# Layer 1's attention put into a written order on three engines, with filler products dealt out by period

## The chip, the core and the metric

One core of one Trainium2 chip runs the whole kernel as one program. The metric is the device time of an execution in microseconds; three executions of the kernel before took 1047.85, 1050.26 and 1059.63 us (median 1050.26).

## The reference

A two-layer decoder trunk on 256 tokens of width 1024, batch 1, in float32. Each layer is half a SwiGLU feed-forward (FFN), a mixer, and another half FFN, each behind an RMS norm that is scaled and shifted from a conditioning vector. The change is in the mixer of layer 1, a sparse attention with 16 heads of 64 in two key/value groups and three branches:

```python
u = h @ in_w                      # q, then k and v of three branches, then gates
q_rope = rope_partial(q, pos)
# compressed branch: 15 blocks of 32 tokens, each through a small MLP
p_c = masked_softmax(q @ kcmp.T * scale, cmp_end <= t);      o_c = p_c @ vcmp
# selected and window branch: at 256 tokens both are causal over all keys
p_s = masked_softmax(q_rope @ ks.T * scale, k <= t);         o_s = p_s @ vs
p_w = masked_softmax(q_rope @ kw.T * scale, k <= t);         o_w = p_w @ vw
y = sum(gate[..., c] * o[c] for c in range(3)) @ out_w
```

With 256 tokens there are four selection blocks and sixteen may be selected, so the selection takes all that are causal; the window of 512 takes all as well.

## The kernel before

All activations lie transposed, channels on the 128 partitions and the 256 tokens along the free axis. Matrix products with weights use two parts of each operand, a rounded high part and the rest: `mm3` (L171) issues high x high, high x low and low x high, three TensorE (PE) products of 128x128 by 128x256. The weights come as tiles of 128x1024 floats by DMA into seven raw buffers (`Stream`, L55 to L114). `need(i)` splits all tiles up to i in the order of one list: ACT makes the high part `wh` (L86), DVE the low part `wl` (L90), and the next DMA is issued. Seven pairs of `wh` and `wl` exist, so a split waits until the tile seven places ahead of it has been used up.

The tile framework's scheduler orders the instructions of each engine. Inside `with in_order()` (L223) PE, DVE and ACT keep the order in which the code is written; two such blocks that follow each other can still be laid into one another by the scheduler.

The mixer of layer 1 (`mixer1`, L937) first projects keys, values, gates and query tiles 0 to 3 (tiles 0 to 7 hold two heads each, one of each group). `rope_q` turns a quarter of each query tile: a DMA gathers the turned rows into `zq`, PE multiplies them with `rot`, DVE takes three steps (L701 to L703), a DMA puts them into `nqr`. `cmp_scores` and `cmp_soft` make the compressed branch's scores and softmax for four tiles at once; `cmp_trans` transposes its weights into `pc`.

Then come eight units u, one per query tile. Both branches and both groups of a unit are worked on together, for two halves t of the queries:

- `score(u, t)`: two products of 64 rows, one per group g, into the banks `s0` or `s1`; two bf16 products add the causal mask; DVE takes the minimum `nm` (L1182). For t = 0 there are 128 keys per branch, for t = 1 there are 256.
- `exps(u, t)`: four exponentials on ACT with their sums (L1193).
- `weights(u)`: reciprocal and gates on DVE (L1198, L1201). `norm(u, t)`: one DVE multiplication (L1206).
- `turn(u, part)`: four transposes on PE into the one bank `pt` (L1215), and a copy into `th`: by ACT for part 0 (L1218), by DVE for parts 1 and 2 (L1220).
- `values(u)`: on PE the compressed values, then sixteen products of `th` with the values into the one bank `y`; then `y` is split into `yh` (ACT, L180) and `yl` (DVE, L181).

Between these stand filler products from a list `todo`: the projections of query tiles 4 to 7 (`q_step`, 96 products), their rotation and compressed softmax, then the output projection (`out_step(b, k)`, six products each, into four accumulators b) as soon as `y[k]` exists. `filler(n)` takes n units of cost from it. None of this is in order by hand: the scheduler decides. What is left of the output projection goes into `step`, called by the next FFN's `transition` (L388). That one is written in order: it first needs the next FFN's five weight tiles (L391), then updates `x` by pairs of accumulators.

Of the kernel before, what the change touches and what calls it, by code (L numbers as in the profile page):

```python
# [18 lines left out]
KD = 8  # L19
# [35 lines left out]
class Stream:  # L55
    def __init__(self, nc, pool, junk, cond, wst, mst, modraw, items, halved):
# [8 lines left out]
        self.n_free = 0  # L65
# [45 lines left out]
    def free(self, i):  # L111
        assert i == self.n_free
        del self.split[i]
        self.n_free += 1  # L114
# [3 lines left out]
def hybrid_trunk_kernel(ctx: ExitStack, tc: tile.TileContext, xT, c, wst, mst, prm_d, cst_d, wab_d, cw1_d, cw2_d,  # L118
# [818 lines left out]
    def mixer1(prev):  # L937
# [132 lines left out]
        def cmp_soft(w):  # L1070
# [8 lines left out]
            A.activation(out=sc, in_=sc, func=ACTF.Exp)  # L1079
            sm = ap.tile([P, 16], F32, tag="csm", name="csm", bufs=2)  # L1080
# [8 lines left out]
            return sc  # L1089
# [21 lines left out]
        sc0 = cmp_soft(0)  # L1111
        att = banks_att()
        late = {}

        def q_step(i, k):
            if k == 0:
                late["b"] = oa()
                late["w"] = st.need(p0 + 7 + i)
                st.need(p0 + 8 + i)
# [29 lines left out]

        todo = [(1, None, lambda i=i, k=k: q_step(i, k)) for i in range(4, 8) for k in range(KD)]  # L1150
        todo += [(1, None, lambda: rope_q(1, ap, oa())), (2, None, cmp1), (0, None, soft1)]
        outs = [(2, k, lambda b=b, k=k: out_step(b, k)) for k0 in (0, 4) for k in range(k0, k0 + 4) for b in range(2)]
        todo += [(1, None, lambda: cmp_trans(1, late["sc"], oa()))] + outs

        def filler(n):
            while todo and n > 0 and (todo[0][1] is None or todo[0][1] in y):
                cost, _, f = todo.pop(0)
                f()
                n -= cost
# [76 lines left out]
        score(0, 0)  # L1236
        exps(0, 0)
        score(0, 1)
        cmp_trans(0, sc0, att("pt", 1))
        filler(8)  # L1240
        for u in range(KD):
            more = 1 if u < 3 else 0
            exps(u, 1)
            if u + 1 < KD:
                score(u + 1, 0)
            filler(3 + more)
            weights(u)
            norm(u, 0)
            if u + 1 < KD:
                exps(u + 1, 0)  # L1250
                score(u + 1, 1)
            turn(u, 0)
            filler(2 + more)
            norm(u, 1)
            turn(u, 1)
            turn(u, 2)
            filler(3 + more)
            values(u)
        gate = gate_of(1, 1)
        params(1, 2)  # L1260
        banks_std()

        def step(b):
            if b == 0:
                filler(100)
                assert not todo
            if b > 1:
# [182 lines left out]
```

## Time and profile before

| | us |
|---|---|
| executions (3) | 1047.85, 1050.26, 1059.63 |
| profiled execution | 1049.2 |
| its span, first to last instruction | 1047.2 |
| granted clock of TensorE, mean | 0.993 of full |
| first score product to last product with the values | 749.83 to 833.81 |

The page lists busy times, shares in 40 slices, the chain of work that ended last, and groups of instructions. "<-" in a row names what was written from what, and a row of the chain gives its start, its length and the engine that held it. [...]

### The profile page before, as it was taken

Reading aid. Unit: us, or ns where it says so; the run is one execution under the profiler, and the core shown is the slowest. Engines: PE = TensorE matmul, PEld = TensorE weight load, DVE = VectorE, ACT = ScalarE, POOL = GpSimd, SP = SyncE. Lnnn points to the kernel's source line nnn. Section 1 sums busy time; section 2 is a strip of 40 time slices with the busy share of each in tenths; the row PEclk is TensorE's granted clock in tenths of the full one; section 3 lists DMA queues with packets and bytes.
Section 4 is the critical chain, followed back from the end, with each engine's and each line's share of the span. In section 5 each row is a group of like instructions: output and inputs, shape, how many; then the busy total and the mean of one; then the engine's idle time right before and its main releaser. Section 6 shows DMA issues by size and latency. Waiting matters only on the chain.

```text
span 1047.2 us, 20415 instructions
## 1 busy us (share of the span) xinstructions
PE 1007.5 (96%) x8102; PEld 961.2 (92%) x8102; DVE 806.8 (77%) x1380; ACT 550.5 (53%) x943; POOL 1.6 (0%) x14
## 2 busy tenths in 40 slices
PE   4999999999999999999999999999999999999997
PEld 2899999999889999999999999998865699999996
DVE  8979887899767988886788888779576578565654
ACT  5364444567966644444674444466744466444442
POOL 0000000000000000000000000000000000000000
PEclk9999999999999999999999999999989999999998
DMA  9989899948543799998359999843620036766611
GB/s 360 336 283 405 313 338 322 360 135 288 209 150 136 268 364 328 332 351 289 121 180 391 332 333 334 321 147 121 222 64 28 17 102 242 264 218 222 225 58 41
DMA packets 69728, 249.99 MB, mean 239 GB/s; under 512 B 8001, under 2 KB 9537, under 8 KB 69378
## 3 DMA queue, kind: packets, MB, share of 16 engines
q1 hardware_dynamic: 69346, 248.18, 66.8%
q8 instruction: 63, 1.03, 0.4%
q10 hardware_dynamic: 288, 0.52, 0.1%
q14 instruction: 31, 0.25, 0.1%
HBM read 245.39 MB, written 1.05 MB: 235 GB/s over the span
## 4 chain that ended last, share of the span: by engine, by line
PE 80%; DVE 10%; ACT 6%; issue 2%; DMA 1%; SPq 0%; ACTq 0%; DVEq 0%
PE ps L169 45%; PE oa L169 17%; PE ob L169 14%; DVE wl L90 2%; PE s L169 2%; PE y L169 2%; ACT wh L86 1%; DVE junk L94 1%; DVE t L460 1%; DVE HL L455 1%; PE pt L1215 1%; DVE x L383 1%; ACT HH L461 1%; DMA raw<-mst 1%; ACT p L1193 1%
## 5 line engine op out<-in xcount | busy, mean ns | idle before, releaser
L90 DVE TENSOR_TENSOR wl<-raw,wh 128x1024 fp32r<-128x1024 f32 (+1 forms) x339 | 384.0, 1147 | 119.6 <-ACT wh L86 118.6
L86 ACT ACTIVATE wh<-raw 128x1024 fp32r<-128x1024 f32 x315 | 328.1, 1055 | 219.2 <-PE ps L169 110.5
L169 PE MATMUL ps<-HL,wh 128*128 128x256 f32 (+1 forms) x1392 | 392.3, 282 | 2.4 <-DVE HL L455 2.4
L169 PE MATMUL ps<-HH,wh 128*128 128x256 f32 (+1 forms) x1392 | 391.7, 283 | 2.7 <-ACT HH L461 2.7
L169 PE MATMUL ps<-HH,wl 128*128 128x256 f32 (+1 forms) x1392 | 393.3, 283 | 0.6 <-DVE wl L90 0.4
L169 PEld LDWEIGHTS ps<-HH,wh 128*128 128x128 f32 x1392 | 262.9, 189 | 4.1 <-ACT HH L461 3.6
L169 PEld LDWEIGHTS ps<-HL,wh 128*128 128x128 f32 x1392 | 262.7, 189 | 3.1 <-DVE HL L455 2.9
L169 PEld LDWEIGHTS ps<-HH,wl 128*128 128x128 f32 x1392 | 264.1, 190 | 1.4 <-DVE wl L90 1.4
L94 DVE SCALAR_TENSOR_TENSOR junk<-raw,cond 128x1024 bf16<-128x1024 f32 x144 | 175.6, 1219 | 12.6 <-DMA raw<-mst 12.5
L169 PE MATMUL oa<-gl,wh 128*128 128x256 f32 x352 | 98.1, 279 | 0.2
L169 PE MATMUL oa<-gh,wh 128*128 128x256 f32 x352 | 98.0, 279 | 0.1
L169 PE MATMUL ob<-gl,wh 128*128 128x256 f32 x352 | 97.7, 278 | 0.1
L169 PE MATMUL oa<-gh,wl 128*128 128x256 f32 x352 | 97.7, 278 | 0.0
L169 PE MATMUL ob<-gh,wh 128*128 128x256 f32 x352 | 97.6, 278 | 0.0
L169 PE MATMUL ob<-gh,wl 128*128 128x256 f32 x352 | 97.5, 277 | 0.0
L180 ACT ACTIVATE gh<-g 128x256 fp32r<-128x256 f32 x82 | 33.6, 417 | 72.9 <-DVE g L489 72.9
L169 PEld LDWEIGHTS oa<-gh,wh 128*128 128x128 f32 x352 | 66.3, 189 | 0.5 <-ACT gh L180 0.5
L169 PEld LDWEIGHTS oa<-gl,wh 128*128 128x128 f32 x352 | 66.2, 188 | 0.5 <-DVE gl L181 0.5
L169 PEld LDWEIGHTS ob<-gl,wh 128*128 128x128 f32 x352 | 66.1, 188 | 0.3 <-DVE gl L181 0.3
L169 PEld LDWEIGHTS oa<-gh,wl 128*128 128x128 f32 x352 | 66.3, 188 | 0.0
L169 PEld LDWEIGHTS ob<-gh,wh 128*128 128x128 f32 x352 | 66.0, 188 | 0.1
L169 PEld LDWEIGHTS ob<-gh,wl 128*128 128x128 f32 x352 | 66.1, 188 | 0.0
(242 smaller groups left out, 1315.1 us busy)
## 6 DMA issues: line engine op xcount, KB each, us to landing
raw<-wst SPq DMA_DIRECT2D x315, 512.0 KB, 5.1
raw<-mst SPq DMA_DIRECT2D x144, 512.0 KB, 5.5
cw<-cw SPq DMA_DIRECT2D x1, 2048.0 KB, 7.6
x<-xT SPq DMA_DIRECT2D x1, 1024.0 KB, 5.2
nqr<-nqf SPq DMA_DIRECT2D x4, 192.0 KB, 3.2
cst<-cst SPq DMA_DIRECT2D x1, 721.0 KB, 7.8
wab<-wab SPq DMA_DIRECT2D x1, 512.0 KB, 4.1
out<-raw ACTq DMA_DIRECT2D x2, 256.0 KB, 3.0
```

The costliest lines, as they stand in the source:

```text
L86: nc.scalar.activation(out=h, in_=raw, func=ACTF.Copy)
L90: nc.vector.tensor_tensor(out=l[:, cols], in0=raw[:, cols], in1=h.bitcast(F32)[:, cols], op=ALU.subtract)
L94: nc.vector.scalar_tensor_tensor(out=self.junk, in0=raw, scalar=1.0, in1=self.cond, op0=ALU.mult, op1=ALU.mult, accum_out=self.modraw[i // ...
L169: PE.matmul(out, lhsT, rhs, start=start, stop=stop, skip_group_check=True)
L180: A.activation(out=h, in_=src, func=ACTF.Copy)
L383: V.scalar_tensor_tensor(out=x[:, d], in0=accs[d // 2][:, d % 2 * S:d % 2 * S + S], scalar=gate[:, d:d + 1], in1=x[:, d], op0=ALU.mult, op ...
L455: V.scalar_tensor_tensor(out=HL[:, k, 0:S], in0=ts.pop(k), scalar=shift[:, k:k + 1], in1=HH[:, k, 0:S].bitcast(F32), op0=ALU.add, op1=ALU. ...
L460: V.scalar_tensor_tensor(out=t, in0=x[:, k], scalar=amp[:, k:k + 1], in1=rbs, op0=ALU.mult, op1=ALU.mult)
L461: A.activation(out=HH[:, k, 0:S], in_=t, func=ACTF.Identity, bias=shift[:, k:k + 1])
L1193: A.activation(out=p[:, 2 * g + br], in_=s[:, g, br * n:br * n + n], func=ACTF.Exp, scale=-1.0, bias=nm[:, g, br:br + 1], accum_out=units[ ...
L1215: PE.transpose(pt[:, c * P:(c + 1) * P], p[:, c, o:o + P], ident)
```

## The change

The whole unit loop goes into one `in_order` block, in periods. Period u writes unit u's scores, minima and exponentials and, between them, unit u-1's transposes; then unit u's `weights` and both `norm`s; then unit u-1's `values`. There are nine periods, the last without a new unit. The fill of a period is a fixed list, cut into three parts: behind transposes 1, behind transposes 2, behind the values. Query tiles 4 to 7 take periods 0 to 2, all 96 products behind the first scores; rotation and compressed softmax period 3; output products the rest, two groups of six per period from period 5 on. The splits are dealt out too: `ahead` says up to which weight tile each period splits, ahead of its `weights`. `cmp_soft` is cut in two, so that the second set's normalization (`cmp_norm`) stands in the next period. Four groups of the third accumulator's output products (`out_step(2, 0..3)`) come behind the last values. Weight tiles may now be freed in any order.

```diff
--- before.py
+++ after.py
@@ -109,9 +108,7 @@
             assert self.step(), "stream blocked"
     def free(self, i):
-        assert i == self.n_free
         del self.split[i]
-        self.n_free += 1
@@ -1077,6 +1074,10 @@
             V.tensor_reduce(out=nmx, in_=sc16, axis=AX.X, op=ALU.max)
             V.tensor_tensor(out=sc16, in0=sc16, in1=nmx.unsqueeze(2).to_broadcast([P, 16, 16]), op=ALU.subtract)
             A.activation(out=sc, in_=sc, func=ACTF.Exp)
+            return sc
+
+        def cmp_norm(w, sc):
+            sc16 = sc.rearrange("p t h c -> p (t h) c")
             sm = ap.tile([P, 16], F32, tag="csm", name="csm", bufs=2)
             V.tensor_reduce(out=sm, in_=sc16, axis=AX.X, op=ALU.add)
             V.reciprocal(out=sm, in_=sm)
@@ -1086,7 +1087,6 @@
                 V.tensor_tensor(out=v, in0=v, in1=gt, op=ALU.mult)
             V.tensor_scalar(out=sm[:, 0:8], in0=sm[:, 0:8], scalar1=C("valid")[:, 0:1], scalar2=None, op0=ALU.mult)
             V.tensor_tensor(out=sc16, in0=sc16, in1=sm.unsqueeze(2).to_broadcast([P, 16, 16]), op=ALU.mult)
-            return sc
 
         def cmp_trans(w, sc, bank):
             scf = sc.rearrange("p t h c -> p (t h c)")
@@ -1109,6 +1109,7 @@
         V.tensor_tensor(out=vb4, in0=bv[:, 0:P].unsqueeze(1).to_broadcast([P, 4, P]),
                         in1=C("vsel").rearrange("p (a d) -> p a d", a=4), op=ALU.mult)
         sc0 = cmp_soft(0)
+        cmp_norm(0, sc0)
         att = banks_att()
         late = {}
 
@@ -1116,7 +1117,6 @@
             if k == 0:
                 late["b"] = oa()
                 late["w"] = st.need(p0 + 7 + i)
-                st.need(p0 + 8 + i)
             b = late["b"][:, 0:S]
             mm3(b, at(late["w"], k), hk(k), k == 0, k == KD - 1)
             if k == KD - 1:
@@ -1146,17 +1146,6 @@
                     k == KD - 1)
             if k % 4 == 3:
                 st.free(wo + i)
-
-        todo = [(1, None, lambda i=i, k=k: q_step(i, k)) for i in range(4, 8) for k in range(KD)]
-        todo += [(1, None, lambda: rope_q(1, ap, oa())), (2, None, cmp1), (0, None, soft1)]
-        outs = [(2, k, lambda b=b, k=k: out_step(b, k)) for k0 in (0, 4) for k in range(k0, k0 + 4) for b in range(2)]
-        todo += [(1, None, lambda: cmp_trans(1, late["sc"], oa()))] + outs
-
-        def filler(n):
-            while todo and n > 0 and (todo[0][1] is None or todo[0][1] in y):
-                cost, _, f = todo.pop(0)
-                f()
-                n -= cost
 
         def scores(u, t):
 
@@ -1233,39 +1222,63 @@
             y[u] = yy
             units[u].clear()
 
-        score(0, 0)
-        exps(0, 0)
-        score(0, 1)
-        cmp_trans(0, sc0, att("pt", 1))
-        filler(8)
-        for u in range(KD):
-            more = 1 if u < 3 else 0
-            exps(u, 1)
-            if u + 1 < KD:
-                score(u + 1, 0)
-            filler(3 + more)
-            weights(u)
-            norm(u, 0)
-            if u + 1 < KD:
-                exps(u + 1, 0)
-                score(u + 1, 1)
-            turn(u, 0)
-            filler(2 + more)
-            norm(u, 1)
-            turn(u, 1)
-            turn(u, 2)
-            filler(3 + more)
-            values(u)
+
+        qs = [lambda i=i, k=k: q_step(i, k) for i in range(4, 8) for k in range(KD)]
+
+        def o(b, k):
+            return lambda: out_step(b, k)
+
+        between = [qs[0:14], qs[14:24], qs[24:32] + [o(0, 0)], [lambda: rope_q(1, ap, oa()), o(0, 1), cmp1, soft1],
...
+        ahead = [2, 3, 5, 5, 5, 7, 7, 8, 8]
+
+        with in_order():
+            st.need(p0 + 12)
+            cmp_trans(0, sc0, att("pt", 1))
+            for u in range(KD + 1):
+                jobs = between[u]
+                n = len(jobs)
+                parts = [jobs[:n // 3], jobs[n // 3:2 * n // 3], jobs[2 * n // 3:]]
+
+                def fill(part):
+                    for f in parts[part]:
+                        f()
+
+                if u < KD:
+                    score(u, 0)
+                if u > 0:
+                    turn(u - 1, 0)
+                if u < KD:
+                    exps(u, 0)
+                    score(u, 1)
+                if u > 0:
+                    turn(u - 1, 1)
+                if u < KD:
+                    exps(u, 1)
+                fill(0)
+                if u > 0:
+                    turn(u - 1, 2)
+                fill(1)
+                st.need(p0 + 11 + ahead[u])
+                if u < KD:
+                    weights(u)
+                    norm(u, 0)
+                    norm(u, 1)
+                if u > 0:
+                    values(u - 1)
+                fill(2)
+            banks_std()
+            for k in range(4):
+                out_step(2, k)
         gate = gate_of(1, 1)
         params(1, 2)
-        banks_std()
 
         def step(b):
-            if b == 0:
-                filler(100)
-                assert not todo
-            if b > 1:
-                for k in range(KD):
+            if b < 2:
+                out_step(b, KD - 1)
+            else:
+                for k in range(4 if b == 2 else 0, KD):
                     out_step(b, k)
             if b == 3:
                 ap_.__exit__(None, None, None)
```

On PE, units 5 and 6 of the kernel before. `s_9836` is the score tile t = 0 of unit 5, `s_9865` that of t = 1; `y` is unit 4's values.

```order
L1215 MATMUL pt<-cst,p 128x128 x2
L169 MATMUL s_9836<-kf,nqr_8993 128x256 x2
L169 LDWEIGHTS identb
L169 MATMUL s_9836<-maskb,identb 128x256
L169 LDWEIGHTS identb
L169 MATMUL s_9836<-maskb,identb 128x256
L1215 MATMUL pt<-cst,p 128x128 x4
L169 MATMUL y<-th,nvp 64x256 x2
L169 MATMUL s_9865<-kf,nqr_8993 128x512
L169 MATMUL y<-th,nvp 64x128 x2
L169 MATMUL y<-th,nvp 64x256 x2
L169 MATMUL y<-th,nvp 64x128 x2
```

The two halves of `s_9865` (x2 where they stand together) are apart: one between the values, the other behind them.

On PE, the same place of the changed kernel: the masks of `s_9930` (unit 6, t = 0) to the fill behind transposes 2.

```order
L166 MATMUL s_9930<-maskb,identb 128x256
L1204 MATMUL pt<-cst,p 128x128 x4
L166 MATMUL s_9950<-kf,nqr_8993 128x512 x2
L166 LDWEIGHTS identb
L166 MATMUL s_9950<-maskb,identb 128x2x128
L166 LDWEIGHTS identb
L166 MATMUL s_9950<-maskb,identb 128x2x128
L1204 MATMUL pt<-cst,p 128x128 x8
L166 MATMUL oa<-yh,wh 128x256
```

The halves stand together, and transposes 1 and 2 follow each other (x8) with no fill between them in periods 5 to 8.

On PE, the head of the stretch in the kernel before, around the compressed scores (`ob<-kbd`); `oa<-HH,wh` and its like are products of query tiles 4 to 7.

```order
L169 MATMUL oa<-HH,wh 128x256
L169 MATMUL oa<-HL,wh 128x256
L169 MATMUL ob<-kbd,nqf_8990 128x32 x8
L169 MATMUL oa<-HH,wl 128x256
L169 MATMUL oa<-HH,wh 128x256
```

The same place of the changed kernel, from the last hidden-layer products (`x_9167`, `hid_9006`) to the first scores.

```order
L166 MATMUL ps<-x_9167,cw_9017 128x2x15 x4
L166 MATMUL ps<-hid_9006,cw_9002 128x32
L166 MATMUL ob<-kbd,nqf_8990 128x32 x8
L166 MATMUL ps<-cw_9002,hid_9306 128x128
L1094 MATMUL pt<-cst,sc 128x128 x2
L166 MATMUL s_9356<-kf,nqr_8992 128x256 x2
```

The 51 query products that stood around the compressed scores are gone from here, and the transpose of the compressed softmax (`pt<-cst,sc`) stands ahead of the first scores.

On DVE, the last unit of the kernel before, from its last minimum to the next FFN's splits.

```order
L1182 TENSOR_REDUCE nm<-s_10027 128x4
L1220 COPY th<-pt 128x4x128 x2
L1198 RECIPROCAL sm<-sm 128x8
L1201 TENSOR_TENSOR sm<-sm,gts 128x4 x2
L1206 TENSOR_TENSOR p<-p,sm 128x512
L1206 TENSOR_TENSOR p<-p,sm 128x1024
L181 TENSOR_TENSOR yl<-y,yh 128x256
L1220 COPY th<-pt 128x4x128 x2
L181 TENSOR_TENSOR yl<-y,yh 128x256
L90 TENSOR_TENSOR wl<-raw,wh 128x1024 x3
```

The same in the changed kernel, from the split that is written in period 7 to the last copy.

```order
L89 TENSOR_TENSOR wl<-raw,wh 128x1024
L1187 RECIPROCAL sm<-sm 128x8
L89 TENSOR_TENSOR wl<-raw,wh 128x1024
L1190 TENSOR_TENSOR sm<-sm,gts 128x4 x2
L89 TENSOR_TENSOR wl<-raw,wh 128x1024
L1195 TENSOR_TENSOR p<-p,sm 128x512
L1195 TENSOR_TENSOR p<-p,sm 128x1024
L178 TENSOR_TENSOR yl<-y,yh 128x256
L89 TENSOR_TENSOR wl<-raw,wh 128x1024
L1209 COPY th<-pt 128x4x128
L89 TENSOR_TENSOR wl<-raw,wh 128x1024
L1209 COPY th<-pt 128x4x128
```

Four splits of later tiles, which stood behind the last unit, are laid by the scheduler between the last unit's steps.

## Rows read from the trace of the kernel before

**Rows 1.** The page: the span, PE's busy time, its granted clock in 40 slices.
```profile
span 1047.2 us, 20415 instructions
...
PE 1007.5 (96%) x8102; PEld 961.2 (92%) x8102; DVE 806.8 (77%) x1380; ACT 550.5 (53%) x943; POOL 1.6 (0%) x14
...
PEclk9999999999999999999999999999989999999998
```

**Rows 2.** Windows of the stretch and its parts.
```profile
core 0: us, PE busy (x) PEld busy (x) DVE busy (x) ACT busy (x) POOL busy (x), PEclk, DMA share, GB/s
749.83:833.62 83.79, 78.15 (x488) 49.96 (x487) 57.57 (x104) 42.30 (x156) 0.00 (x0) 0.96 0.18 58
...
776.40:786.60 10.20, 8.68 (x47) 6.33 (x46) 6.51 (x15) 3.83 (x17) 0.00 (x0) 0.68 0.42 117
...
802.46:833.83 31.37, 28.74 (x196) 18.37 (x196) 20.46 (x35) 14.52 (x51) 0.00 (x0) 1.00 0.10 34
741.50:749.83 8.33, 8.33 (x72) 8.19 (x72) 2.15 (x6) 4.80 (x10) 0.00 (x0) 1.00 0.89 335
```

**Rows 3.** The chain that ended last: start us, length us, what.
```profile
775.62 0.37 ACT nqf L969
...
776.69 2.35 DMA zq<-nqf
...
798.28 1.94 ACT p L1193 x7
...
800.27 1.12 PE s L169 x2
...
802.41 1.05 PE s L169 x2
...
809.76 1.13 PE s L169 x4
...
824.24 0.67 PE pt L1215 x4
...
824.94 0.70 DVE th L1220
...
831.46 0.44 PE pt L1215 x4
831.90 1.91 PE y L169 x18
...
836.29 5.55 PE ob L169 x47
...
841.86 1.07 ACT wh L86
```

**Rows 4.** Instructions by shape, 749.83 to 833.62: busy us, mean ns, idle before.
```profile
L1182 DVE TENSOR_REDUCE nm<-s 128x4 f32<-128x1024 f32 x8 | 9.7, 1214 | 5.1 <-PE s L169 5.1
L1206 DVE TENSOR_TENSOR p<-p,sm 128x1024 f32<-128x1024 f32 x8 | 9.7, 1211 | 0.0
L90 DVE TENSOR_TENSOR wl<-raw,wh 128x1024 fp32r<-128x1024 f32 x7 | 8.5, 1220 | 3.1 <-ACT wh L86 3.1
...
L86 ACT ACTIVATE wh<-raw 128x1024 fp32r<-128x1024 f32 x6 | 6.2, 1051 | 2.6 <-PE oa L169 2.6
L1206 DVE TENSOR_TENSOR p<-p,sm 128x512 f32<-128x512 f32 x8 | 5.5, 692 | 0.0
```

**Rows 5.** Timeline of the head, and of a lone half of tile 0.
```profile
742.80 0.36 ACT L1101 ACTIVATE kbd<-ps 64x16 f32<-64x16 f32 x2
...
745.11 1.87 PE L169 MATMUL ob<-kbd,nqf 128*128 128x32 f32 x16
...
793.17 0.70 PE L169 MATMUL s<-kf,nqr 64*128 64x256 f32 x2
793.80 0.39 PE L169 MATMUL s<-maskb,identb 128*128 128x256 bf16 x2
```

More of the change, by code (lines that the diff above doesn't have):

```diff
@@ L64, in __init__ @@
         self.split = {}
-        self.n_free = 0
         self.done_m = set()
@@ new lines, in o @@
+        def o(b, k):
+            return lambda: out_step(b, k)
+        between = [qs[0:14], qs[14:24], qs[24:32] + [o(0, 0)], [lambda: rope_q(1, ap, oa()), o(0, 1), cmp1, soft1],
+                   [o(1, 0), lambda: cmp_norm(1, late["sc"]), o(1, 1), o(0, 2), o(1, 2), lambda: cmp_trans(1, late["sc"], att("pt", 1))]]
+        between += [[o(0, k), o(1, k)] for k in range(3, 7)]
+        ahead = [2, 3, 5, 5, 5, 7, 7, 8, 8]
[35 more added lines that the diff above has]
+                out_step(2, k)
```

## The prediction

> **What bounds the kernel now.** I read the page first, then the windows of the stretch, the chain of waits, the instructions by shape and the timeline. The page says that TensorE (PE) counts as busy for 96% of a span of 1047.2 us, at full granted clock but for one slice inside [rows 1]. The change touches one stretch, from the first score product at 749.83 to the last product with the values, which ends at 833.81 with its drain of 0.2 [rows 3]: 83.8 us, 8% of the span. There PE counts as busy for 78.2 us, DVE for 57.6, ACT for 42.3 [rows 2]. PE's figure says too much, since a product counts until its last column is out. Its work can be counted from dense rows. One of the 174 projection products that the changed stretch holds takes 5.55/47 = 0.118 us; a pair of score halves 0.63 us (tile 0) or 1.13 (tile 1), with masks some 0.78 and 1.27; four transposes 0.44; a unit's products with the values 1.9 [rows 3, 5]. Eight units: 8 x (0.78 + 1.27 + 3 x 0.44 + 1.9) = 42.2. 174 products: 20.5. Rotation, compressed scores and their transposes: some 2.5. Together 65 us. Whatever the order, the rest of the stretch is waits between PE, DVE and ACT, and that is what a new order can win or lose.
>
> Three things in the order of before cost PE time. A lone score half costs what the pair costs: 1.12 and 1.05 us for two instructions against 1.13 for four [rows 3], and 0.63 for a lone half of tile 0 (793.17 to 793.80) [rows 5]. Around the eighth query tile the chain leaves PE at 775.62: read-out, DMA issue and DMA until 779.04, 3.4 us [rows 3]. Soon after, the granted clock falls: it averages 0.68 over 776.40 to 786.60, so 10.2 x 0.32 = 3.3 us of PE time go [rows 2].
>
> **The change part by part.** *Score halves.* Nine of the sixteen score tiles of before have their halves apart, five large and four small; all stand together now. That is 5 x 1.05 + 4 x 0.63 = 7.8 us of PE time, won only where PE is what ends last.
>
> *Rotation.* The eighth query tile is now complete at the end of unit 2's period, and the rotation comes after unit 3's scores, about 3 us later. The trip of 3.4 us lies beside them almost whole, and the next transposes wait longer there anyway. I price it at nothing.
>
> *Head.* Before, 51 projection products (6.0 us) stood between the hidden-layer products at 741.5 and the first scores, beside ACT's table loads and the compressed softmax; PE was busy for all of that window [rows 2]. Now all 96 come after the first scores, and the first thing after the compressed scores is the transpose of the finished softmax. So the head is the bare chain: the keys are ready at 742.80 + 0.36, the compressed scores take 1.87 [rows 5], drain 0.2, and ten small operations of DVE and ACT follow, with ten hand-overs of 0.03 to 0.04 (as from 824.91 to 824.94 in rows 3). They are smaller than the 128x512 that takes 0.69 [rows 4], eight of them with 256 columns or fewer; I estimate 0.4 for each, 3.9 together, and put the first scores at 749.6. That is only 0.2 earlier than before, with 6.0 us of work still to do.
>
> *One period per unit.* In a period PE runs scores 0 of unit u, transposes 0 of u-1, scores 1, transposes 1, fill, transposes 2, fill, values of u-1, fill. Transposes 2 need the bank that DVE's copy 1 empties, and that copy stands on DVE behind the minimum over the large scores. Up to there the path is 0.78 + 0.44 + 1.27 + 0.2 drain + 1.21 (the minimum) + 0.69 (the copy) + 0.5 (transposes from a standstill), 5.1 us with hand-overs and with DVE's next instruction starting 0.08 before the last ends [rows 3, 4]; then 1.9 for the values, and 0.118 for each product placed behind transposes 2. A product before them is free up to 14 (PE waits 1.65 us there). So a period is 7.0 us plus its later fill.
> Unit 0: scores 2.05 and 42 products: 7.0.
> Unit 1: 7.0 + 21 x 0.118, and 1.2 of waiting: the split of a weight tile stands ahead of the softmax weights, and ACT's half of it behind the read-out of query tile 4. That is scores 2.05, 24 products 2.8, read-out behind the exponentials until 5.8, then 1.05 and 1.22 for the split [rows 4], 0.4 for reciprocal and gates, 0.69 for norm 0: 9.0, and PE is there at 7.8. So 10.7.
> Unit 2: 9.4. Unit 3: 6 products, compressed scores 1.87, and 0.5 from three rotation steps on DVE ahead of copy 2: 10.1. Unit 4: 18 products and two transposes, 9.3. Unit 5: 12 products, 8.5. Unit 6: the same plus 1.0, because two splits (ACT's half behind the exponentials) stand ahead of unit 5's norms: 9.5. Unit 7: 8.5. Sum 73.0.
>
> *Last unit.* DVE's queue in unit 7 is the worst place of the order. Besides the split written there, two of the next stage's stand between the reciprocal and the first norm, and two more between the copies. The large minimum ends 3.9 us into the period, the large exponentials take 1.94 [rows 3], and ACT's three halves end at 6.9, 7.9 and 8.9; DVE's end at 8.1, 9.4 and 10.7, norm 0 at 11.4. PE runs dry at 8.5, so it waits 2.8. Then transposes and copies come one by one with a split between them: about 1.4 (0.70 of transposes and 0.6 of the copy on ACT), 1.9, 1.4, and 1.9 for the values. So 9.4, and the values of unit 7 end 73.0 + 9.4 = 82.4 us after the first scores, at 832.0, against 833.6. Gain 1.6.
>
> *Tail.* The split that the next stage needs first (its fifth tile) waits for output products to free its buffer. It starts at 841.86 [rows 3], 8.25 after the values. Now 7 + 24 + 11 + 24 = 66 products stand there, the first 30 of which cover unit 7's read-out: 66 x 0.118 + 0.2 = 8.0. Gain 0.25. Behind it the order is as before.
>
> *Clock.* Not shown at the new places, so bounded. The rows show one fall, after the chain had been off PE for 3.4 us, and a loss of 3.3 us. The head now has 743.2 to 749.6 with 2.2 us of work, and the end of unit 7 some 6 us with four short groups. Each place costs between 0 (as in 802.46 to 833.83, where the clock stays at 1.00 [rows 2]) and 3.3. I take half, 1.65, at each: a fall that starts while nothing runs spends part of itself on nothing.
> [...]
>
> **The sum.** -1.6 - 0.25 + 3.3 = +1.45 on the profiled execution's 1049.2 us: 1050.7. That execution stands 1.1 below the median of the three runs (1050.26; 1047.85 to 1059.63).
>
> A cross-check: 7.8 (halves) + 3.4 (rotation) + 3.3 (clock) - 6.0 (head) = 8.5 us could be won. 82.4 - 65 = 17.4 us of waits in the new order stand against 83.8 less the old order's work, which is 65 - 5.3 (45 products fewer) + 7.8: 16.3, of which 6.7 were rotation and clock, so 9.6 against 17.4. That leaves 0.7, near the 1.6.
>
> **Rivals.**
> 1. *The clock holds at both places.* For it: PE never stands quite bare for longer than about 4 us; against it: the fall of before came after 3.4. 1049.2 - 1.85 = 1047.4.
> 2. *The clock is low through periods 5 to 7* (slower). Their fill is only 12 products, and PE waits 1.65 us in each 8.4 at the same place. If that is enough, 6.4 us of each path double in three periods (+19), and the time is about 1069. It decides from the point at which a window between 797 and 824 shows under 0.9. Against it: 802.46 to 833.83 held 1.00 with 28.7 of 31.4 counted busy [rows 2].
> 3. *The waits overlap*, because hand-overs are shorter than I count or the engines run further ahead: PE's own work becomes the bound. At the full 65 us the time is 1049.2 - 83.8 + 65 = 1030; half of the way 1039. Against it: the path of a period is a chain of dependent instructions with measured times.
> 4. *The second trip of the rotation is late.* Rotated queries go to unit 4 by DMA from DVE's last rotation step, 32.9 us after the start; with the first trip's 3.4 they are there at 36.3, and unit 4 starts at 37. If the trip is twice as long, 1050.7 + 2.7 = 1053.4.
> That the order isn't what it says is excluded, since the three engines' orders are listed; only the two blocks' overlap in the last unit departs from the written order, and it is priced.
>
> **How the numbers follow.** Forecast (the clock falls at one or both places) 0.62, own range 1046 to 1055. Rival 1: 0.20. Rival 2: 0.07. Rival 3 beyond 1%: 0.05. Rival 4: 0.06. About 1% (10.5 us) is what a measurement of this kernel can tell from no change. Faster comes from rival 3 alone: 0.05. Slower from rival 2 and a hundredth for a sum that fails elsewhere: 0.08. Within 1%: 0.87. The range takes in rival 1 with the last unit's splits harmless (1047.4 - 2.8 = 1044.6, so 1044) and both falls at 3.3 with rival 4 (1047.4 + 6.6 + 2.7 = 1056.7, so 1057).
>
> **What would show it.** Right: no lone score half; 82 to 87 us from the first scores to the last values; in each of periods 5 to 7 a wait of PE of 1.2 to 1.7 us for DVE's copy 1; 2 to 3 us before unit 7's first transposes, on the norm; a granted clock under 1 near 750 and near 830, and nowhere between. Wrong: a stretch under 78 us (the waits overlap), a fall between 760 and 820, unit 4's scores waiting for a DMA, or the fifth split starting much later than 8 us after the last values.

## The result, and the profile after

The changed kernel takes 1060.48 us (median of 20 executions, 1055.77 to 1068.07), the kernel before 1049.86 in the same comparison (20 executions). The ratio is 1.0096, 95% interval 1.007 to 1.0122: slower by about 1%, where the prediction said 1050.7 and a range up to 1057. (The ratio leaves disturbed executions out, such as one of before that took 3438 us; the medians here and below are over all.) The profiled execution took 1057.26 us, 3.2 below its median, as that of before stood below its own.

First the page of the changed kernel, for [rows 1]:

```profile
span 1055.4 us, 20400 instructions
...
PE 1001.9 (95%) x8102; PEld 961.2 (91%) x8102; DVE 807.5 (77%) x1380; ACT 549.7 (52%) x943; POOL 1.6 (0%) x14
...
PEclk9999999999999999999999999999799899999999
```

The span is 8.2 us longer while PE's busy time is 5.6 us shorter: the same 8102 instructions on PE run, and the lone score halves are gone as planned. So the loss must be standing time and clock. The clock row has a 7 where the head of the stretch lies and an 8 at the end of unit 7; before it had an 8 at the rotation and one in the last slice.

Now the stretch by periods: windows of the changed kernel from the first scores of one unit to those of the next; the eighth window ends where PE runs dry in unit 7, and the ninth with the values of unit 7. The three rows behind the dots are the first fall of the clock, the time between the falls, and the second fall. Columns as in [rows 2]: length, then busy time of each engine, then PEclk.

```profile
core 0: us, PE busy (x) PEld busy (x) DVE busy (x) ACT busy (x) POOL busy (x), PEclk, DMA share, GB/s
752.20:761.61 9.41, 9.41 (x55) 6.66 (x54) 2.53 (x3) 5.04 (x19) 0.00 (x0) 0.76 0.01 2
761.61:772.42 10.81, 9.74 (x73) 7.04 (x72) 8.42 (x16) 5.64 (x20) 0.00 (x0) 1.00 0.19 58
772.42:782.36 9.94, 9.53 (x73) 7.12 (x72) 7.12 (x12) 6.96 (x22) 0.00 (x0) 1.00 0.19 61
782.36:793.67 11.31, 8.79 (x67) 6.37 (x66) 8.74 (x16) 4.41 (x18) 0.00 (x0) 1.00 0.44 139
793.67:803.45 9.78, 9.01 (x70) 6.56 (x69) 8.29 (x19) 4.61 (x19) 0.00 (x0) 1.00 0.00 0
803.45:812.29 8.84, 7.36 (x55) 4.92 (x54) 4.99 (x6) 6.58 (x21) 0.00 (x0) 1.00 0.01 2
812.29:822.04 9.75, 7.55 (x55) 4.87 (x54) 8.75 (x17) 4.30 (x18) 0.00 (x0) 1.00 0.33 108
822.04:830.96 8.92, 7.44 (x55) 4.93 (x54) 5.13 (x8) 6.76 (x21) 0.00 (x0) 1.00 0.00 0
830.96:842.44 11.48, 7.20 (x37) 5.04 (x37) 7.47 (x11) 2.75 (x4) 0.00 (x0) 0.70 0.69 230
...
743.09:756.74 13.65, 9.34 (x34) 6.12 (x35) 4.50 (x13) 4.35 (x16) 0.00 (x0) 0.50 0.11 44
756.74:835.25 78.51, 65.30 (x488) 47.37 (x488) 57.38 (x98) 45.19 (x152) 0.00 (x0) 1.00 0.20 63
835.25:842.08 6.83, 5.83 (x29) 4.05 (x29) 3.18 (x4) 0.00 (x0) 0.00 (x0) 0.50 0.67 225
```

Read the first column against the forecast: 7.0, 10.7, 9.4, 10.1, 9.3, 8.5, 9.5, 8.5 and 9.4. Six of the nine windows are within 0.6 us. The three that are not: the first (+2.4), unit 3 (+1.2) and the end (+2.1); and the first scores stand at 752.2, not 749.6 (+2.6). Unit 3 is at full clock; the other three places lie in or touch the two windows with a PEclk of 0.50, which are the whole of the two falls. The whole stretch, from 752.20 to 842.44, is 90.2 us long, outside the 82 to 87 that the prediction gave as a sign of being right.

The chain of waits shows what the half clock does to the same work (start, length, what), for [rows 3, 5]:

```profile
743.62 3.62 PE ob L166 x16
747.25 0.60 PE ps L166 x2
...
747.87 0.69 DVE vb L1109
...
751.04 0.44 DVE sc L1089
751.48 0.14 issue
751.62 0.66 PE pt L1094 x2
752.27 4.26 PE s L166 x12
...
756.55 1.24 DVE nm L1171
...
782.28 0.63 SPq L705
...
782.96 5.07 DMA zq<-nqf
788.03 0.14 issue
788.17 0.67 PE oa L166 x2
...
836.66 1.12 PE pt L1204 x4
837.78 1.28 PE oa L166 x6
839.06 3.38 PE y L166 x18
842.44 1.02 PE oa L166 x7
```

The compressed scores take 3.62 us where they took 1.87 [rows 5]; unit 0's twelve score products 4.26, where two pairs cost 0.78 + 1.27 = 2.05; the last values 3.38 where they took 1.91 [rows 3]. PE's waits in the stretch (engine, line, waited for: us in all, times, longest) name the rest:

```profile
PE pt L1204 <- DVE th L1209: 7.0, 7, 1.5
PE pt L1204 <- DVE p L1195: 4.0, 3, 2.6
PE pt L1094 <- DVE sc L1089: 3.8, 1, 3.8
PE oa L166 <- DMA zq<-nqf: 2.5, 1, 2.5
PE ob L166 <- ACT kbd L1101: 1.5, 1, 1.5
```

The 1.5 on copy 1 and the 2.6 ahead of unit 7's transposes are the waits that were forecast. The 2.5 on the rotation's DMA is not. In the head the fall begins at 743.09, within the wait of 1.5 us (1.48, until 743.62) and ahead of the 3.8, which lies inside the fall.

**Time against clock.** The 20 executions of this one program spread over 12 us. The granted clock has two levels here, 0.50 and 1.00 in the windows above, so 2 x (1 - mean clock) x span is the time spent at the lower one; call it low-clock time. Part of it, 4 to 8 us in the profiled executions (5.1 in the changed kernel, 7.7 in before), lies at the very end of the span. In the changed kernel it runs from 21.1 us (in the execution of 1055.77) to 51.2 (1068.07), with a median of 33.9, and a straight line, 1047.0 + 0.414 x low-clock time, fits the 20 executions with a correlation of 0.99. For 29 executions of before (those beside the first four experiments) the median is 14.7 and the line 1044.8 + 0.418 x low-clock time. So of the 10.6 us between the medians 0.42 x (33.9 - 14.7) = 8.1 go with the clock, and 2 to 2.5 with the order itself. That is a correlation, and the experiments put it to the test.

### The profile page after: what moved, and what is told of

Its sections match the earlier page's. It is cut to its first block, busy times and chain, and to the rows that moved or that the text cites. A ratio compares the mean times of both kernels' runs of the same rounds, so it can differ in the third digit from the quotient of the medians.

```text
span 1055.4 us, 20400 instructions
## 1 busy us (share of the span) xinstructions
PE 1001.9 (95%) x8102; PEld 961.2 (91%) x8102; DVE 807.5 (77%) x1380; ACT 549.7 (52%) x943; POOL 1.6 (0%) x14
## 4 chain that ended last, share of the span: by engine, by line
PE 80%; DVE 10%; ACT 6%; issue 2%; DMA 1%; SPq 0%; ACTq 0%; DVEq 0%
PE ps L166 45%; PE oa L166 17%; PE ob L166 14%; DVE wl L89 2%; ACT wh L85 2%; PE s L166 2%; PE y L166 2%; DVE junk L93 1%; DVE t L457 1%; DVE HL L452 1%; DVE x L380 1%; DVE nm L1171 1%; ACT HH L458 1%; ACT p L1182 1%; PE pt L1204 1%
## 5 line engine op out<-in xcount | busy, mean ns | idle before, releaser
L85 ACT ACTIVATE wh<-raw 128x1024 fp32r<-128x1024 f32 x315 | 327.8, 1055 | 214.4 <-PE ps L166 104.7
```

The costliest lines, as they stand in the source:

```text
L85: nc.scalar.activation(out=h, in_=raw, func=ACTF.Copy)
```

## The experiments

Theory A: the loss is the clock, which falls at the two places that the new order leaves bare (the head before the first scores, and the end of unit 7). Theory B: the waits of the written order are the loss, and the low clock only goes with them. All runs were timed in five rounds beside the kernel before, whose medians were 1050.14 (first four runs, 29 executions), 1050.39 (next four, 35) and 1050.69 (last three, 29). The last column takes 0.42 x low-clock time off each execution, and is the median of what is left; the slopes fitted for single kernels ran from 0.37 to 0.475, so it is good to about 1 us. The clocks are on record to 0.001, so low-clock time comes in steps of 2.1 us.

| kernel | executions | median us | ratio to before, 95% | low-clock us, median | less 0.42 x low clock |
|---|---|---|---|---|---|
| before | 29 | 1050.14 | | 14.7 | 1044.8 |
| the change | 20 | 1060.48 | 1.0096 (1.007 to 1.0122) | 33.9 | 1046.8 |
| e1_hold_head | 12 | 1057.12 | 1.0079 (1.0039 to 1.0119) | 21.1 | 1048.4 |
| e2_no_hoist | 12 | 1056.55 | 1.005 (1.0019 to 1.0082) | 26.4 | 1045.7 |
| e3_q_head | 6 | 1062.53 | 1.011 (1.0071 to 1.0148) | 30.8 | 1049.7 |
| e4_zq | 12 | 1057.11 | 1.0061 (1.0029 to 1.0094) | 27.4 | 1045.5 |
| e5_hold_both | 12 | 1053.36 | 1.0013 (0.9975 to 1.0051) | 10.5 | 1048.5 |
| e6_trans_late | 12 | 1056.91 | 1.0047 (1.0011 to 1.0082) | 27.4 | 1044.7 |
| e7_best | 12 | 1046.33 | 0.9961 (0.9921 to 1.0001) | 16.7 | 1040.1 |
| e8_bare_head | 12 | 1056.03 | 1.0031 (0.9995 to 1.0068) | 23.2 | 1046.5 |
| e9_best_q6 | 12 | 1047.21 | 0.9949 (0.9916 to 0.9982) | 14.6 | 1041.1 |
| e10_fill | 12 | 1057.33 | 1.0059 (1.0027 to 1.0091) | 26.4 | 1045.9 |
| e11_best_hold | 12 | 1048.65 | 0.9965 (0.9937 to 0.9992) | 13.6 | 1043.5 |

The changed kernel was not timed again beside the experiments, so a comparison with it goes by its own set of executions. e1, e2, e4, e6 and e10, edits of quite different kinds, all stand 3.2 to 3.9 us below it, and the intervals of their ratios overlap with its own. A gain of that size over the change can't be put down to the edit by the time alone. e5, e7, e9 and e11 are clear of it: their intervals end at 1.0051 or below, and its own begins at 1.007.

### Keeping PE going at the bare places

e1_hold_head, an edit of the changed kernel:

```diff
+        def hold(n, o):
+            for _ in range(n):
+                mm(o, HH[:, 0, 0:P], HH[:, 1, 0:S], True, True)
+
+        idle = oa()[:, 0:S]
+        hold(10, idle)
         bk = ps()
...
             st.need(p0 + 12)
+            for _ in range(8):
+                mm(idle, hid4.rearrange("p a c -> p (a c)"), qf[0][:, 0], True, True)
```

> The changed kernel with 18 products more in the head (10 behind the last hidden-layer product, 8 behind the compressed scores), into a bank that nobody reads: work for PE that brings nothing. Theory A, the loss is the granted clock that falls at the bare places: no fall between 743 and 757, first large minimum at about 752 instead of 756.6, 4 us less than the changed kernel (about 1056.5), and 13 us less time at the low clock. Theory B, the loss is the waits of the written order itself and the clock only goes with them: within 1 us of the changed kernel, 1060.

1057.12, with 17 to 21 us of low-clock time in eight of the twelve executions; those took 1055.4 to 1057.7. In three of the others it was 47 to 49 and the time about 1069. The profiled execution is one of those three, and its fall began at 731.0, before the first idle product, and lasted 30.72 us. The median is 3.4 us under the change's although work was added, which theory B did not expect. But the intervals of the two ratios overlap, so the time alone doesn't settle it. Against a fall that had already begun, as in the profiled execution, the idle products did not help.

e5_hold_both covers the end of unit 7 as well (`hold` as above, here into a free score bank):

```diff
+                if u == KD:
+                    idle = att("s0", 2)[:, 0, 0:S]
+                    hold(20, idle)
                 if u > 0:
                     turn(u - 1, 0)
+                if u == KD:
+                    hold(8, idle)
...
                 fill(0)
+                if u == KD:
+                    hold(8, idle)
                 if u > 0:
                     turn(u - 1, 2)
```

> The changed kernel with products whose results nobody reads at both bare places: 10 ahead of the key product and 8 after the compressed scores (as in e1_hold_head), and 20, 8 and 8 ahead of unit 7's first, second and third transposes. They bring nothing to the output. Theory A (the loss is the granted clock, falling at the two bare places): the head's fall and the fall near 835 both stay away or get shorter, low-clock time 8 to 12 us instead of about 33, and 1052 to 1054. Theory B (the loss is the waits of the written order): the waits stay as they are, 1057 as with the head alone, or more, since the idle products can hold up the transposes.

1053.36, with 10.5 us of low-clock time: both numbers as theory A had them, and the interval of the ratio lies below the change's. Not one written wait was removed; 54 products whose results nobody reads were added, and they give back 7 of the 10.6 us. The profiled execution (1064.64) had the early fall again, but its end of unit 7 stayed at full clock. Its windows, first the early fall and then the end of unit 7 (columns as above):

```profile
731.13:761.85 30.72, 30.26 (x125) 29.20 (x125) 5.02 (x16) 7.75 (x15) 0.00 (x0) 0.50 0.24 75
...
839.00:850.00 11.00, 10.68 (x91) 9.26 (x88) 8.96 (x14) 4.65 (x7) 0.00 (x0) 1.00 0.71 234
```

And its chain in the second of them:

```profile
846.20 0.66 PE pt L1211 x4
846.86 0.71 PE oa L166 x6
847.57 1.88 PE y L166 x18
```

0.66, 0.71 and 1.88 stand where the changed kernel has 1.12, 1.28 and 3.38: the same three groups, 2.5 us shorter. Its last column in the table, 1048.5, is 1.7 above the changed kernel's, so by that column the idle products cost some 1.7 us, and the clock gives back more.

### The bare head alone, in the kernel before

e8_bare_head:

```diff
-        score(0, 0)
-        exps(0, 0)
-        score(0, 1)
-        cmp_trans(0, sc0, att("pt", 1))
-        filler(8)
+        with in_order():
+            cmp_trans(0, sc0, att("pt", 1))
+            score(0, 0)
+            exps(0, 0)
+            score(0, 1)
+            filler(8)
```

> The kernel before, with the first scores' block written so that the transposes of the compressed softmax stand ahead of the first scores, as in the change; all the rest is ordered as before. It makes the head bare, without periods. Theory A: a fall of the clock of 7 to 20 us appears near 743 to 755, and the time is 1055 to 1059. Theory B: the clock is not what costs; the head loses only what it waits, at most 3.8 us, and the scheduler fills it in part: about 1050 to 1052.

1056.03. Here is the fall in its head as a window, in a kernel that has none of the new periods:

```profile
744.47:758.12 13.65, 9.88 (x36) 5.66 (x36) 5.49 (x13) 5.20 (x14) 0.00 (x0) 0.50 0.00 1
```

And PE's waits from 742 to 760:

```profile
PE pt L1094 <- DVE sc L1088: 3.8, 1, 3.8
PE ob L169 <- ACT kbd L1101: 1.5, 1, 1.5
```

The same two waits, 3.8 and 1.5, stand with a fall of the same 13.65 us as in the changed kernel. (With the same waits it lasted 10.24 us in e2_no_hoist's profiled execution.) Low-clock time went from 14.7 to 23.2, which is 3.6 of the 5.6 us lost between the medians; that the rest, about 2, is the head's own wait is argued. Theory A by the time and the fall. The interval reaches just below 1, so the time alone would not decide it.

### The end of unit 7 and the rotation

e2_no_hoist keeps the splits of the next stage out of unit 7 (`+ st.need(p0 + 23)` behind the last values).

> The changed kernel with the splits of four later weight tiles written behind the last values, so that none is laid between the last unit's steps. Theory B: PE's wait of 2.6 us for unit 7's first norm goes, and 1 us between the copies: 1057. Theory A: the same, and with it the clock's fall at 835 for another 2 us: 1055.

1056.55, 3.9 below the change; the wait of 2.6 us ahead of unit 7's transposes went down to 0.7, and low-clock time from 33.9 to 26.4 (3.2 us). With the clock taken off, the gain is about 1 us; the rest goes with the clock. In the profiled execution the fall at the end of unit 7 lasted 3.41 us instead of 6.83, but falls of 3.41 came at two other places, and the low-clock time in all is the change's (25.3 us in both). B's number was nearer (1057 against 1055), and this run does not decide between the theories.

e4_zq moves one weight split from period 2 to period 3:

```diff
-        ahead = [2, 3, 5, 5, 5, 7, 7, 8, 8]
+        ahead = [2, 3, 4, 5, 5, 7, 7, 8, 8]
```

> The changed kernel with the split of one weight tile moved from period 2 to period 3, so that fewer weight DMAs stand ahead of the rotation's DMA on SP's queue. If that queue made the trip late (5.1 us instead of 2.4), PE's wait of 2.5 us at 785 shrinks to under 1.3 and the time by about 1.3 us, to 1059; if the DMA itself is slow there, nothing changes. Theories A and B say the same here.

1057.11, 3.4 below the change. With the clock taken off, 1.3 of it is left, which is the gain that was expected; the rest goes with low-clock time, which this edit was not meant to alter. Why a split matters to the rotation is seen in SP's queue: its timeline in the changed kernel, and behind it that of this run.

```profile
740.34 41.85 SPq L71 DMA_DIRECT2D raw<-wst  x6
782.28 1.29 SPq L705 DMA_DIRECT2D zq<-nqf  x2
```

```profile
786.41 0.33 SPq L71 DMA_DIRECT2D raw<-wst  x1
787.84 1.29 SPq L705 DMA_DIRECT2D zq<-nqf  x2
```

In the change SP stands at a weight load behind the second split of period 2, which DVE ends at 781.84 (the profile has the load released at 782.16). The query DMA is queued behind it and goes out at 782.28, 0.14 us after ACT has read out the last columns that it needs (781.76 + 0.38). It takes 5.07 us, against 2.35 [rows 3]; over the 5.07 the DMA engines are busy for 0.76 and move 235 GB/s, over the 2.35 in the kernel before it was 0.50 and 103. That the weight loads beside it make it slow is argued from this. With the split one period later the load goes out at 786.41 and the query DMA 1.43 us behind it, at 787.84; PE does not wait for it any more, and in place of the 2.52 us PE waits 1.04 there, for copy 1. How SP stands in its queue is seen in the row of the change: the six loads stretch over 41.85 us, with single waits of up to 21.1, and no other DMA of SP goes out among them.

### Reordering the head

e3_q_head moves 51 query products ahead of the written block, and deals the other 45 over periods 0 to 2:

```diff
+        for f in qs[0:17]:
+            f()
         with in_order():
-            st.need(p0 + 12)
+            st.need(p0 + 13)
```

> The changed kernel with 51 of the query products back ahead of the written block, where the scheduler lays them into the head as before; the other 45 are dealt over periods 0 to 2. Theory A: no fall in the head (4 us), and 21 products fewer behind transposes 2 in periods 1 and 2 (2.5 us): about 1054. Theory B: the 2.5 us alone, 1058.

1062.53: no faster than the change, against both theories. The transposes of the compressed softmax still came ahead of the first scores (a wait of 2.2 us), PE then waited 2.0 and 1.7 us for weight splits that were now needed earlier, and 3.1 for the rotation. The run says nothing on the clock; it shows that products can be brought forward only as far as their weights are split.

e6_trans_late moves the first tile's compressed softmax and its transposes into period 0:

```diff
-        cmp_norm(0, sc0)
...
-            cmp_trans(0, sc0, att("pt", 1))
...
+                if u == 0:
+                    cmp_norm(0, sc0)
                 fill(0)
...
                 fill(2)
+                if u == 0:
+                    cmp_trans(0, sc0, att("pt", 1))
```

> The changed kernel with the first tile's compressed softmax and its transposes moved from the head into period 0, so that unit 0's scores follow the compressed scores directly. Theory A: the bare head is gone; the first large minimum stands about 7 us earlier (near 749 instead of 756.5) and no fall of the clock begins between 740 and 760, so the last values stand some 6 us earlier and the time is about 1051. Theory B: the order of the head alone costs its wait of 3.8 us and some, the clock being a side matter: about 1056.

1056.91. The first large minimum came 5.1 us earlier (751.46), but the fall did not go: it began at 746.13 and lasted 6.83 us in the profiled execution, half as long, with others of 3.41 at the rotation and behind the stretch, and 6.83 at the end of unit 7. Theory A's 1051 failed. What is left of the bare head are two waits between small products, one of 1.5 us that ends at 744.02, ahead of the fall, and one of 0.8 inside it; that the first is enough to start a fall is argued, from where it stands. The fall as a window (columns as above):

```profile
746.13:752.96 6.83, 6.05 (x23) 3.24 (x22) 3.87 (x7) 2.16 (x10) 0.00 (x0) 0.50 0.00 0
```

Of the 3.6 us gained on the change 2.7 go with the clock (6.5 us less) and 1 to 2 with the order.

e10_fill puts one of two output groups ahead of the third transposes in periods 5 to 8:

```diff
                 parts = [jobs[:n // 3], jobs[n // 3:2 * n // 3], jobs[2 * n // 3:]]
+                if n == 2:
+                    parts = [jobs[:1], [], jobs[1:]]
```

> The changed kernel with one edit alone: in periods 5 to 8 the first of the two output groups is placed ahead of the third transposes instead of behind the values, into the wait of 1.5 us for the copy. By the step 'one period per unit' a product ahead of the third transposes is free up to 14 of them, so 6 products a period move from a paid place to a free one: 6 x 0.118 = 0.7 us in each of periods 5 to 7, some 2 to 2.5 us in all, the falls of the clock as in the changed kernel: about 1058. If the periods are set by something else (softmax weights, ACT), 1060 as the changed kernel.

1057.33 where 1058 was expected. In the trace the waits on copy 1 fell from 1.48 to 0.77 us, exactly the 0.7 per period of the forecast's model, but the wait for unit 7's norm grew from 2.60 to 3.30. What the periods gain, the last unit gives back where DVE sets the pace. Most of the difference in time to the change goes with low-clock time (26.4 against 33.9), which the edit wasn't meant to alter; that part is not explained.

### Repairs together

e7_best has e6, e2, e4 and e10 in one.

> The changed kernel with four repairs: the compressed softmax of the first tile in period 0 (e6), no splits hoisted into unit 7 (e2), one split moved out of the rotation's way (e4), and one fill group ahead of the third transposes in periods 5 to 8. Theory A and the ledger of the waits together: 1043 to 1046, below both kernels. Theory B: the periods still set the stretch (7.0 us each plus the fill behind it), about 1050.

1046.33, 14.2 us under the change and 4.1 under before. Its windows, the whole of the head's fall and all up to the next fall:

```profile
742.75:752.99 10.24, 8.71 (x32) 5.80 (x33) 2.94 (x7) 4.17 (x16) 0.00 (x0) 0.50 0.16 65
753.00:1039.00 286.00, 272.45 (x2244) 252.10 (x2242) 192.85 (x307) 146.22 (x305) 0.00 (x0) 1.00 0.43 145
```

The fall at the end of unit 7 is gone, that of the head isn't. Less clock the kernel is at 1040.1, 6.7 below the change; the four repairs alone made 2.1, 1.1, 1.3 and 0.9, together 5.4, so within the 1 us of each they add up. The other 7.2 us go with 17 us less of low-clock time. The 95% interval reaches 1.0001, so this run by itself does not settle that it beats the kernel before.

e9_best_q6 fills the head's gap of 1.5 us with products that are needed anyway:

```diff
+        for f in qs[0:6]:
+            f()
         with in_order():
...
-        between = [qs[0:14], qs[14:24], qs[24:32] + [o(0, 0)], [lambda: rope_q(1, ap, oa()), o(0, 1), cmp1, soft1],
+        between = [qs[6:16], qs[16:25], qs[25:32] + [o(0, 0)], [lambda: rope_q(1, ap, oa()), o(0, 1), cmp1, soft1],
```

> e7_best with 18 query products of the next stage (2.1 us of TensorE) moved from the first three periods into the gap of 1.49 us ahead of the compressed scores. Theory A: useful work covers the last wait of the head; the first large minimum stands about 0.6 us later, the periods 0 to 2 get some 1 us shorter, and the low-clock time of the head (10.24 us in e7_best) falls to 7 us or less: 1044 to 1045.5. Theory B (only waits count, the clock does not answer to such a cover): no shorter fall, 1046 as e7_best.

1047.21, with 14.6 us of low-clock time: no better than e7_best, so the expectation was missed, though the gap was gone from the trace. (Its profiled execution has a fall from 732.49 to 746.14, which covers the place of the gap, so the trace doesn't show what the fill did to the head's own fall.) Its ratio, 0.9949 with an interval of 0.9916 to 0.9982, is the best settled gain of the set: this order does beat the kernel before, by half a per cent.

e11_best_hold is e7_best with the idle products of e1_hold_head.

> e7_best with the idle products of e1_hold_head (10 ahead of the key product, 8 after the compressed scores; they bring nothing to the output). Theory A: they cost about 1.2 us of time without clock (as e5_hold_both against the changed kernel, 1048.2 against 1047.0) and take the head's fall away (10.24 us x 0.42 = 4.3 us): low-clock time about 6 us instead of 14.6, time about 1043 to 1044.5. Theory B: 1047.5, the idle products cost and nothing comes back.

1048.65: missed. In the profiled execution the head stayed at full clock (731 to 760: PEclk 1.00), as theory A says, but there were falls of 3.41 us at 827.41 and 851.30, and the idle products cost some 3.4 us of their own, not 1.2. The window of the head, and the twelve score products of unit 0 in the chain:

```profile
731.00:760.00 29.00, 27.84 (x204) 24.75 (x205) 10.59 (x24) 12.92 (x35) 0.00 (x0) 1.00 0.29 89
...
749.91 2.35 PE s L166 x12
```

The twelve take 2.35 us where they took 4.26 in the changed kernel. Theory A tells where a fall is cured; it doesn't tell where others come.

## Why the prediction was wrong

The steps by their names in the prediction:

- *Score halves*: right. PE's busy time fell by 5.6 us although some 7 us of its work were stretched by the clock.
- *One period per unit*: right in kind, short in size. Units 1, 2 and 4 to 7 came within 0.6 us of their forecasts, which were 2.1 short in sum, and PE's wait for copy 1 was 1.48 in periods 5 to 7 (forecast 1.2 to 1.7). e10_fill's trace agrees that products ahead of the third transposes are free: six of them there made PE's wait 0.7 us shorter.
- *Last unit*: right but for the clock. PE ran dry for 2.60 us (forecast 2.8). The end took 11.48 us against 9.4, and three groups at half clock cost 2.5 more than at full clock.
- *Tail*: right. From the last values at 842.44 to the fifth split at 850.52 it is 8.08 us (forecast 8.0).
- *Head*: the chain was right, the time wasn't. The small operations from 747.87 to 751.48 took 3.6 us (forecast 3.9), but the compressed scores ran at half clock: 3.62 - 1.87 = 1.75, and the product and the transposes behind them some 0.5 more (an estimate: 0.60 and 0.66 us at half clock, against 0.30 in e11_best_hold's chain and the 0.44 of four transposes [rows 3]). The keys were 0.4 us later, too, than in the rows.
- *Rotation*, "I price it at nothing": wrong, by some 1.2 us (unit 3's window). The step looked at DVE, ACT and PE and forgot what else SP had in its queue. The wait moved from 0.6 us in the order before to 2.5.
- *Clock*, "each place costs between 0 ... and 3.3. I take half, 1.65, at each": this is the step that failed. The places were right: low near 750 and near 830, full clock between. The price was not. In the profiled execution the head's fall costs about 2.2 us up to the first scores and 2.2 in them, and the end's 2.5: 6.9 in all, 3.6 more than the 3.3 in the sum. (By the 2.35 us of e11_best_hold the second figure is 1.9, and the total 6.6.) The head's 4.4 are above the 3.3 that the step gave as the most for one place; the end's 2.5 are not. And that is one of the cheaper executions: it has 25.3 us of low-clock time where the median has 33.9, and the missing 8.6 x 0.414 = 3.6 us are about the 3.2 by which the median is higher; at which places the median execution has them no trace shows. The row on which the bound rested [rows 2] priced one fall in one execution, and was taken as the most that any fall can cost. Here is that fall in the kernel before, and PE's waits ahead of it:

```profile
780.05:786.88 6.83, 6.83 (x36) 5.15 (x36) 3.60 (x11) 0.73 (x3) 0.00 (x0) 0.50 0.33 107
...
777.93 0.66 PE L1215 MATMUL pt<-cst,p 128*128 128x128 f32 x4 [0.93 <-ACT th L1218]
779.18 0.67 PE L169 MATMUL oa<-zq,cst 128*128 128x256 f32 x2 [0.59 <-DMA zq<-nqf]
```

It lasted 6.83 us; the head's lasted 13.65. And the 3.4 us "off PE" were the chain's, not PE's: PE itself had stood for 0.93 and 0.59 us. So the trace of before already had a fall behind much shorter waits than the step and rival 1 supposed.

Sum: 1050.7, with 3.6 for the clock and 1.2 for the rotation, is 1055.5; the 2.1 by which the periods were short make it 1057.6, against 1057.26 in the profiled execution. So of the 6.6 us by which that execution missed the forecast about half is the clock's price and about half are waits, 1.2 and 2.1 us.

How the loss against the kernel before is shared between clock and order is known only roughly. Between the profiled executions, 8.1 us apart, the clock makes 6.9 - 3.3 = 3.6 and the order 4.5. Between the medians, 10.6 apart, the fitted line gives the clock 8.1, and the table's last column gives the order 2.0 (1046.8 against 1044.8). The prediction, with its clock terms left out, had 1.5 for the order (1047.4 against 1045.9). That this is near the 2.0 is in part luck, since the sum had missed 3.3 us of waits.

Of the rivals, 1 (the clock holds) is what e5_hold_both comes near to by force; 2 (low through periods 5 to 7, with paths that double, as the 0.50 in the window of before has it) did not come, since 756.74 to 835.25 held 1.00; 3 (the waits overlap) did not come. What rival 4 had, a trip twice as long, did come, but on the first trip of the rotation, not on the second. The forecast's chance of 0.87 for no measurable change rested on a range of the clock's price that was too narrow, when the one thing that it could not read from rows was what a second and a third bare place cost.

## What to carry to other kernels

Before work is moved out of a place where an engine stood covered, price the bare place twice: the wait, and what TensorE loses on the work behind it if its clock falls (here 0.42 us for each us at the lower level, and falls of 3 to 30 us). Judge such a change by the mean granted clock of every execution as well as by the time: time against low-clock time separates the order from the clock roughly, with a handful of executions. Time the kernel that the experiments are compared with again beside them. And when a DMA is moved, read what is queued ahead of it on its issuing engine, and what releases that.

## What the runs showed of the hardware that was not expected

- One program has very different low-clock times: 21.1 to 51.2 us over 20 executions of the change, 8.4 to 42.4 over the 29 of before. In the profiled executions of the two it lies in the middle and at the end: from 743.09 to 756.74, 835.25 to 842.08 and 1050.3 on in the change, from 780.05 to 786.88 and 1039.5 on in before. All else stands at 1.00, the first 700 us in both.
- A fall can begin while PE counts as busy. In e9_best_q6's profiled execution (1052.63 us) it does so within the products of the hidden layer (windows, columns as above):

```profile
732.49:746.14 13.65, 13.65 (x60) 13.47 (x59) 1.06 (x3) 2.76 (x3) 0.00 (x0) 0.50 0.28 79
```

PE is busy for all of the 13.65 us. It had stood for 0.83 us until 730.07; the changed kernel and the one before have the same stand at that place (0.83 and 0.81 us), and their profiles hold 1.00 from there until 743.09 and 780.05. Which property of the work there brings it about was not tried.
- A wait of the same length can have a fall behind it or none. Behind the stretch, ahead of the same four products, e7_best and e11_best_hold (first and second row) have this:

```profile
849.19 0.61 PE L166 MATMUL ob<-over_d,sqs 128*128 128x1 f32 x4 [1.58 <-DVE sqs L353]
850.05 0.61 PE L166 MATMUL ob<-over_d,sqs 128*128 128x1 f32 x4 [1.57 <-DVE sqs L353]
```

e7_best stays at 1.00; in e11_best_hold a fall of 3.41 us begins at 851.30. The profiles of e2, e6, e8 and e10, too, have a fall of 3.41 behind this wait, so it is not shown that e11's came of its covered head. What decides whether a fall starts stays open.
